# Wide projections of a hybrid GLA/HGRN2 layer: four blocks of 256 columns per job, 512 columns per matmul, in tile pools of their own

## Chip, cores and metric

The kernel runs on one core of one Trainium2 chip. The metric is device time of one execution in microseconds (us), the median of several runs. TensorE is called PE below (its weight loads PEld), VectorE DVE, ScalarE ACT, GpSimd POOL, and SyncE, which issues most of the DMAs, SP.

## What is computed

The reference is one encoder layer on 1024 tokens of width 1024, all in float32. What matters here is its first line: one large projection, whose column blocks are used in different ways.

```
p = jnp.einsum('btd,dp->btp', h, w_in)
(a_q, a_k, a_v, a_gate, a_lr_f, a_lr_b,
 h_q, h_f_f, h_f_b, h_i, h_gate, m_gla, m_hgrn) = _split_columns(p)
...
o_a = head_rmsnorm(o_a, gla_norm_g).reshape(B, T, GLA_V) * jax.nn.silu(a_gate)
y_gla = o_a @ w_branch_gla
...
o_h = head_rmsnorm(o_h, hgrn_norm_g).reshape(B, T, HG_V) * jax.nn.silu(h_gate)
y_hgrn = o_h @ w_branch_hgrn
y = jax.nn.sigmoid(m_gla) * y_gla + jax.nn.sigmoid(m_hgrn) * y_hgrn
return layer_norm(DEEPNORM_ALPHA * h + y @ w_out, ln_g, ln_b)
```

Between the projection and the norms stand two bidirectional chunked recurrences: 4 GLA heads and 8 HGRN2 heads. The four blocks `a_gate`, `h_gate`, `a_v` and `h_i`, 1024 columns each, are the wide projections: their results are wanted with tokens on the partitions.

## The kernel before

**Numbers.** A float32 product is made of three matmuls of the rounded type float32r: each operand is split into a high part (a cast on ACT, line 91) and a low part, what the cast left over (a subtraction on DVE, line 92), and high*high, high*low and low*high are added up in PSUM. So a product over 4 blocks of 128 inner elements takes 12 matmuls for each tile of its output.

**Seven products.** The projection uses Strassen's scheme in Winograd's form. Inputs, tokens and columns are each cut in two, and instead of eight products of quarter size seven are made, P1 to P7, from sums of operand quarters (`sums`) and with sums of results (`seven`, line 1012 for the additions). All seven operands on the side of x are kept in SBUF (`xs`).

**Stage one** is `dense`. It runs 16 narrow jobs and then eight wide ones, and builds the operands of job n+1 (`prepare`) ahead of job n. A narrow job makes two blocks of 128 columns, with weights as the stationary operand and 512 tokens streaming (`narrow_product`, line 975). A wide job makes two blocks of 256 columns, with 128 tokens stationary and 256 columns of weights streaming (`wide_product`, line 988): 7 products of 4 token blocks of 12 matmuls. With the last eight narrow jobs go the GLA decays, one `gla_logs` each: two matmuls (line 1167), then a chain of four ACT passes (lines 1168 to 1171, with two loads of activation tables), three DVE steps (lines 1169, 1172 and the running sum of line 1180) and a store. Halves of the merge gates (`merge_half`, 24 matmuls of 512 columns at line 1315) stand at the start of the stage (0 to 5) and at its end (6 to 8, `STARTED` to `BEGUN`).

**Stage two** is `heads`: 12 heads in the order of `SEQUENCE`, with the rest of the merge gates (`MERGES`, line 1375) and later the GLA branch as work that fills PE in between; a merge gate below `BEGUN` needs one half more, the others both. Stage three is the HGRN branch and the last product (lines 1375 and 1635).

**Order and memory.** The tile framework schedules the instructions of each engine in advance; an engine then runs its queue strictly in that order, and SP its DMAs too. Loads go through SP, in stage one stores go through POOL. Each stage has pools of its own in SBUF, `p0` here: `runs`, `raw` (5 tiles), `s` (3), `w` (8) and `h` (13). When a stage's pools close, the next stage's lie over them, and a new tile waits until the old tiles under it are done with. PSUM has eight banks of 512 columns (`bank`).

Of the kernel before, what the change touches and what calls it, by code (L numbers as in the profile page):

```python
# [9 lines left out]
F32 = mybir.dt.float32  # L10
# [6 lines left out]
P = 128  # L17
# [857 lines left out]
class Fast(Layer):  # L875
# [106 lines left out]
    def wide_product(self, w, x):  # L982
        def product(out, name, more=False):
            a, b = w[name], x[name]
            terms = [(k, i, j) for k in range(4) for i, j in ((0, 0), (1, 0), (0, 1))]
            for c in range(4):
                for n, (k, i, j) in enumerate(terms):
                    self.nc.tensor.matmul(  # L988
                        out[c // 2][:, 256 * (c % 2) : 256 * (c % 2) + 256],
                        b[k][:, j, P * c : P * c + P],  # L990
                        a[i][:, k, :],
                        start=(n == 0 and c % 2 == 0 and not more),
                        stop=(n == len(terms) - 1),
                        skip_group_check=True,
                    )

        return product

# [214 lines left out]
    def wide_job(self, kind, columns, w):  # L1213
        nc = self.nc
        for column in columns:
            self.staged[column] = self.dr.tile([P, NT * 256], F32, name=f"{kind}d")

        def out(i, j, n, c, psum):
            o = 1024 * j + 512 * n
            s = c  # L1220
            if kind == "gate":
                s = self.h()
                nc.scalar.activation(s, c, AF.Sigmoid)
                nc.vector.tensor_tensor(out=s, in0=c, in1=s, op=ALU.mult)
            elif psum:
                s = self.h()
                nc.scalar.copy(s, c)
            self.store(self.staged[columns[i]][:, o : o + 512], s)

        self.seven(self.wide_product(w, self.xs), 2, out)  # L1230

    def dense(self):
# [11 lines left out]
        self.staged = {}  # L1244
# [13 lines left out]
        def block(column):  # L1258
            halves = []
            for n in range(2):  # L1260
                r = self.t("raw", (P, 4, 256))
# [547 lines left out]
```

## Time and profile before

| | us |
|---|---|
| median of three runs | 1408.28 |
| the three runs | 1407.91, 1408.28, 1414.06 |
| the profiled execution | 1407.21 |
| its span | 1405.5 |
| PE busy | 1333.9 |
| DVE busy | 867.5 |
| ACT busy | 670.9 |

The profile is of one execution. A busy PE is not a PE at its peak: matmuls overlap, and what a stream of them costs is read from its length divided by their number, not from the duration of one. The chain of waits is followed back from the last instruction: at each step to what released it. A gap of an engine that the chain doesn't pass costs nothing.

### The profile page before, as it was taken

What the parts mean: (1) busy time and instruction counts of PE and PEld (TensorE: products, weight loads), DVE (VectorE), ACT (ScalarE), POOL (GpSimd) and SP (SyncE); (2) the same over time, 40 slices, a digit from 0 to 9 for tenths busy, and PEclk for the clock granted to TensorE, in tenths of its full rate; (3) what the DMA queues carried; (4) which work ended last, traced back from release to release, by engine and by line L of the source; (5) the groups of instructions that cost most, each with busy time, mean ns of one, the idle gap of its engine ahead of it and who ended that gap; (6) DMA issues with size and microseconds to landing.
All of it is one profiled execution on the core that took longest, in us unless ns stands there. A gap on an engine that the chain in (4) does not pass through costs nothing.

```text
span 1405.5 us, 21115 instructions
## 1 busy us (share of the span) xinstructions
PE 1333.9 (95%) x8009; PEld 1150.1 (82%) x8009; DVE 867.5 (62%) x1434; ACT 670.9 (48%) x1190; POOL 172.6 (12%) x270
## 2 busy tenths in 40 slices
PE   7999989999989999999999999998889999799996
PEld 5888867777889999999987888776677888577885
DVE  8787775797666666444435565567666354675544
ACT  6566565766533333222214565576766455654100
POOL 1134342111111111110010000001000000000011
PEclk9999989999999999999999999999899999899999
DMA  7343433343342333333266353455766241775431
GB/s 277 120 173 137 148 135 119 114 142 120 143 158 97 99 98 121 105 106 111 92 239 221 107 200 112 166 184 191 237 220 211 82 135 53 271 261 172 158 102 52
DMA packets 83153, 210.45 MB, mean 150 GB/s; under 512 B 10656, under 2 KB 10656, under 8 KB 80992
## 3 DMA queue, kind: packets, MB, share of 16 engines
q1 hardware_dynamic: 68368, 160.48, 33.7%
q0 software_dynamic: 14672, 48.51, 9.1%
q8 instruction: 65, 1.06, 0.3%
q14 instruction: 48, 0.39, 0.1%
HBM read 137.65 MB, written 71.30 MB: 149 GB/s over the span
## 4 chain that ended last, share of the span: by engine, by line
PE 74%; DMA 11%; ACT 6%; DVE 5%; issue 3%; POOL 1%; SPq 0%; POOLq 0%; DVEq 0%; ACTq 0%
PE bank L988 22%; PE bank L975 16%; PE proj L1375 13%; PE bank L1635 6%; PE po L566 5%; PE st L566 3%; PE sc L382 2%; DMA raw<-in_dram 2%; PE bank L1315 2%; DMA PF<-logs 2%; DMA hraw<-in_dram 2%; PE bank L1375 2%; DMA g<-ua 1%; DMA g<-sigs 1%; DMA oa<-ot 1%
## 5 line engine op out<-in xcount | busy, mean ns | idle before, releaser
L975 PE MATMUL bank<-xP,w 128*128 128x512 f32 x1344 | 316.9, 396 | 13.5 <-DVE h L1012 8.1
L988 PEld LDWEIGHTS bank<-w,xP 128*128 128x128 f32 x2688 | 323.6, 192 | 0.4
L988 PE MATMUL bank<-w,xP 128*128 128x256 f32 x2688 | 323.5, 283 | 0.0
L975 PEld LDWEIGHTS bank<-xP,w 128*128 128x128 f32 x1344 | 255.3, 191 | 71.5 <-DVE h L1012 9.6
L1375 PE MATMUL proj<-x,hw 128*128 128x512 f32 x576 | 148.5, 402 | 3.0 <-ACT hw L91 1.6
L91 ACT CAST w<-s 128x512 fp32r<-128x512 f32 (+1 forms) x96 | 72.6, 761 | 122.0 <-PE bank L988 71.9
L91 ACT CAST w<-raw 128x512 fp32r<-128x512 f32 (+1 forms) x90 | 65.1, 731 | 131.9 <-PE bank L988 90.7
L1375 PEld LDWEIGHTS proj<-x,hw 128*128 128x128 f32 x576 | 106.1, 190 | 25.1 <-DVE hw L92 1.9
L92 DVE TENSOR_TENSOR w<-s,w 128x512 fp32r<-128x512 f32 (+1 forms) x96 | 83.9, 876 | 56.9 <-ACT w L91 56.7
L1375 PE MATMUL bank<-oh,hw 128*128 128x512 f32 x384 | 91.7, 400 | 9.8 <-ACT hw L91 7.9
L1375 PEld LDWEIGHTS bank<-oh,hw 128*128 128x128 f32 x384 | 73.3, 193 | 28.0 <-ACT hw L91 8.6
L1375 PE MATMUL proj<-xP,hw 128*128 128x512 f32 x360 | 94.3, 402 | 2.0 <-ACT hw L91 1.6
L1012 DVE TENSOR_TENSOR h<-bank,h 128x512 f32<-128x512 f32 x96 | 65.7, 686 | 42.8 <-PE bank L988 35.2
L1528 POOL TENSOR_TENSOR rs<-msall,mhalf 128x4 f32<-128x4 f32 (+1 forms) x32 | 28.4, 887 | 441.2 <-DVE msall L1527 434.8
L92 DVE TENSOR_TENSOR hw<-hraw,hw 128x512 fp32r<-128x512 f32 x64 | 44.0, 688 | 62.2 <-ACT hw L91 62.0
L92 DVE TENSOR_TENSOR w<-raw,w 128x512 fp32r<-128x512 f32 (+1 forms) x90 | 74.7, 837 | 11.9 <-ACT w L91 10.9
L1375 PEld LDWEIGHTS proj<-xP,hw 128*128 128x128 f32 x360 | 65.4, 188 | 17.4 <-ACT hw L91 2.5
L1012 DVE TENSOR_TENSOR h<-h,bank 128x512 f32<-128x512 f32 x65 | 44.5, 685 | 53.7 <-PE bank L988 30.0
L1565 ACT ACTIVATE V<-st,ends 128x128 f32<-128x128 f32 (+1 forms) x168 | 58.4, 421 | 18.9 <-PE st L566 18.7
L566 PE MATMUL st<-v,KT 128*128 128x128 f32 (+1 forms) x336 | 61.0, 324 | 5.5 <-ACT V L1565 5.1
L1315 PE MATMUL bank<-xP,w 128*128 128x512 f32 x216 | 53.8, 412 | 7.9 <-ACT xP L91 6.8
L91 ACT CAST hw<-hraw 128x512 fp32r<-128x512 f32 x64 | 39.8, 623 | 42.9 <-PE proj L1375 25.5
(194 smaller groups left out, 2011.9 us busy)
## 6 DMA issues: line engine op xcount, KB each, us to landing
raw<-in_dram SPq DMA_DIRECT2D x82, 256.0 KB, 3.1
hraw<-in_dram SPq DMA_DIRECT2D x68, 256.0 KB, 3.3
raw<-in_dram SPq DMA_DIRECT2D x33, 512.0 KB, 3.7
ks<-h POOLq DMA_DIRECT2D x40, 256.0 KB, 3.1
K<-ks SPq DMA_DIRECT2D x20, 512.0 KB, 4.8
logs<-h POOLq DMA_DIRECT2D x32, 256.0 KB, 2.7
gated<-h POOLq DMA_DIRECT2D x32, 256.0 KB, 2.7
vd<-h POOLq DMA_DIRECT2D x32, 256.0 KB, 2.7
```

What stands on the lines that cost most here:

```text
L91: nc.scalar.copy(hi, raw)
L92: (lo_engine or nc.gpsimd).tensor_tensor(out=lo, in0=raw, in1=hi.bitcast(F32), op=ALU.subtract)
L382: mm = lambda out, l, r: nc.tensor.matmul(out, l, r, start=True, stop=True)
L566: self.nc.tensor.matmul(out, l, r, start=(i == 0), stop=(i == len(terms) - 1))
L975: self.nc.tensor.matmul(out[0], a[i][:, k, :], b[k][:, j, :], start=(n == 0 and not more), stop=(n == len(terms) - 1), skip_group_check=True,)
L988: self.nc.tensor.matmul(out[c // 2][:, 256 * (c % 2) : 256 * (c % 2) + 256], b[k][:, j, P * c : P * c + P], a[i][:, k, :], start=(n == 0 a ...
L1012: nc.vector.tensor_tensor(out=to[n], in0=one[n], in1=two[n], op=op)
L1315: self.nc.tensor.matmul(ps, w.both[a][:, k, :], xs[k][:, b, :], start=(m == 0), stop=(m == len(terms) - 1))
L1375: nc.tensor.matmul(ps, parts[k][a], self.plain[k, n][:, b, :], start=(m == 0), stop=(m == len(terms) - 1))
L1528: nc.gpsimd.tensor_tensor(out=rs[:, cs], in0=ms, in1=self.mhalf[:, cs], op=ALU.pow)
L1565: nc.scalar.mul(new, u, ends[:, c, near : near + 1])
L1635: nc.tensor.matmul(pss[m], y[:, k, rows], self.wo[k, n][:, j, part], start=(i == 0), stop=(i == len(terms) - 1))
```

## The change

The eight wide jobs become four (`quad_job`), each of four blocks of 256 columns: one quarter of the weights is now 512 columns wide, and a matmul streams 512 columns into a whole bank. The four jobs run in a stage of their own (`wide_stage`, line 1266 for the matmuls), in pools of their own over those of `dense`: `blk` (5 tiles of 4 x 512), `w` (6 tiles, one for each inner block, high and low together), `h` (12) and `g` (2). A product takes its four banks in turn, inner block by inner block; only P3, the last, goes bank by bank. The sums of weights are built in place in `blk` (line 1212). Results are staged with two blocks side by side, so that a store has pieces of 256 elements. The order of the jobs is gate, gate, H_I, A_V instead of gate, gate, A_V, H_I. One more half of a merge gate is made ahead of the heads (four in place of three: 6 in `dense`, 7 to 9 in `wide_stage`), and `MERGES` is shifted by one.

```
-        for start, kind, n in ((A_GATE, "gate", 4), (H_GATE, "gate", 4), (A_V, "v", 4), (H_I, "v", 4)):
-            for b in range(0, n, 2):
-                jobs.append((kind, None, (start + 256 * b, start + 256 * (b + 1))))
...
+    def quad_operands(self, columns):
...
+        def load(i, n):
+            r = block()
+            for m in range(2):
+                src = self.io["ww"][WIDE.index(columns[2 * i + m])]
+                nc.sync.dma_start(out=r[:, :, 256 * m : 256 * m + 256], in_=src[:, 4 * n : 4 * n + 4, :])
+            return r
...
+        def put(raw):
+            tiles = []
+            for k in range(4):
+                u = self.t("w", (P, 2, 512), F32R)
+                self.split(u[:, 0], u[:, 1], raw[:, k])
+                tiles.append(u)
+            return tiles
+
+        a11, a21, a22, a12 = load(0, 0), load(1, 0), load(1, 1), load(0, 1)
+        yield put(a11)
+        s1 = block()
+        sub(s1, a21, a22, ALU.add)
+        sub(a21, a11, a21)
+        sub(a11, s1, a11)
+        yield put(a11)
+        yield put(a12)
+        sub(a12, a12, a11)
+        yield put(a21)
+        yield put(s1)
+        yield put(a22)
+        yield put(a12)
...
+        def out(i, j, n, c, psum):
+            o = 1024 * j + 256 * n
+            s = c
+            if kind == "gate":
+                s = self.t("g", (P, 512))
+                nc.scalar.activation(s, c, AF.Sigmoid)
+                to = s if psum else c
+                nc.vector.tensor_tensor(out=to, in0=c, in1=s, op=ALU.mult)
+                s = to
...
+            self.store(self.pairs[columns[2 * i]][:, :, o : o + 256], s.rearrange("p (m e) -> p m e", e=256))
+
+        def product(banks, name, w, more=False, last=False):
+            terms = [(k, i, j) for k in range(4) for i, j in ((0, 0), (0, 1), (1, 0))]
+            turns = [(c, n) for n in range(len(terms)) for c in range(4)]
+            if last:
+                turns.sort()
+            for c, n in turns:
+                k, i, j = terms[n]
+                nc.tensor.matmul(
+                    banks[c],
+                    self.xs[name][k][:, j, P * c : P * c + P],
+                    w[k][:, i],
...
+    def wide_stage(self):
+        self.counts = {"blk": 5, "w": 6, "h": 12, "g": 2}
+        self.staged, self.pairs = {}, {}
+        for start, kind in ((A_GATE, "gate"), (H_GATE, "gate"), (H_I, "v"), (A_V, "v")):
+            self.quad_job(kind, [start + 256 * b for b in range(4)])
+        for i in range(self.JOINED, self.BEGUN):
+            self.merge_half(i)
...
-        for i in range(self.STARTED, self.BEGUN):
+        for i in range(self.STARTED, self.JOINED):
             self.merge_half(i)
...
-    STARTED, BEGUN = 6, 9
+    STARTED, JOINED, BEGUN = 6, 7, 10
...
-    MERGES = ((9, 10), (11, 0), (12, 1), (13, 2), (14, 3), (15, 4), (5, 6), (7, 8), (), (), (), ())
+    MERGES = ((10, 0), (11, 1), (12, 2), (13, 3), (14, 4), (15, 5), (6, 7), (8, 9), (), (), (), ())
...
-                    self.stage(c, "p0", [["runs"], ["raw"], ["s"], ["w"], ["h"]])
-                    self.dense()
+                    with ExitStack() as n:
+                        self.stage(n, "p0", [["runs"], ["raw"], ["s"], ["w"], ["h"]])
+                        self.dense()
+                    with ExitStack() as n:
+                        self.stage(n, "p0w", [["blk"], ["w"], ["h"], ["g"]])
+                        self.wide_stage()
```

**Place one: PE, from the last narrow job into the wide ones.** The two matmuls of line 1167 are those of the last `gla_logs`; line 975 with xP_160 is the narrow P2, with xP_430 P7, with xP_269 P3; line 988 is a wide matmul. Before:

```order
L1167 MATMUL bank<-w 128x512 x2
L988 MATMUL bank<-w,xP_134 128x256 x2
L975 MATMUL bank<-xP_160,w 128x512 x3
L975 MATMUL bank<-xP_161,w 128x512 x3
L975 MATMUL bank<-xP_162,w 128x512 x3
L975 MATMUL bank<-xP_163,w 128x512 x3
L988 MATMUL bank<-w,xP_134 128x256 x2
L975 MATMUL bank<-xP_430,w 128x512 x3
L975 MATMUL bank<-xP_431,w 128x512 x3
L975 MATMUL bank<-xP_432,w 128x512 x3
L975 MATMUL bank<-xP_433,w 128x512 x3
L988 MATMUL bank<-w,xP_135 128x256 x3
```

In the changed kernel the same two matmuls and the 24 of P2 and P7 follow each other without any wide ones, and then come (line 1393 is a half of a merge gate, line 1266 a wide matmul):

```order
L1393 MATMUL bank<-xP_160,w 128x512 x3
L1393 MATMUL bank<-xP_161,w 128x512 x3
L1393 MATMUL bank<-xP_162,w 128x512 x3
L1393 MATMUL bank<-xP_163,w 128x512 x3
L975 MATMUL bank<-xP_269,w 128x512 x3
L975 MATMUL bank<-xP_270,w 128x512 x3
L975 MATMUL bank<-xP_271,w 128x512 x3
L975 MATMUL bank<-xP_272,w 128x512 x3
L1266 MATMUL bank<-w,xP_134 128x512 x12
L1266 MATMUL bank<-w,xP_135 128x512 x12
L1266 MATMUL bank<-w,xP_136 128x512 x12
```

What fills PE between the last decays and the wide jobs is now 24 matmuls of merge gate 6 and no longer the first wide products, which stand behind all of the narrow stage.

**Place two: SP, the loads of weights at the same point.** The names in brackets are the semaphores that a load waits for: DMASW for a store through POOL, DMAHW for an earlier load. Before, the first wide loads take `raw` tiles in turn:

```order
L1059 DMA raw_2866<-in_2_dram 128x512 [waits DMASW2_49,DVE_49]
L1059 DMA raw_2866<-in_2_dram 128x512
L1262 DMA raw_3023<-in_3_dram 128x1024 [waits DMAHW1_49,DMAHW6_49,DMAHW0_49,DVE_49]
L1262 DMA raw_3025<-in_3_dram 128x1024 [waits DMAHW3_49,DMAHW2_49,DMAHW7_49,DVE_49,Activation_49]
L1262 DMA raw_3027<-in_3_dram 128x1024 [waits DMASW7_49,DVE_49]
L1262 DMA raw_3029<-in_3_dram 128x1024 [waits DMAHW5_49,DMAHW4_49,DVE_49]
```

In the changed kernel (`raw_3144` is merge gate 6, `blk_3222` is a11, `blk_3225` a21, `blk_3228` a22):

```order
L1379 DMA raw_3144<-in_2_dram 128x512 [waits DMAHW6_49,DMASW7_49,DVE_49]
L1379 DMA raw_3144<-in_2_dram 128x512 [waits DMAHW7_49]
L1207 DMA blk_3222<-in_3_dram 128x4x256 [waits DMASW7_49,DMAHW0_49,DMASW2_49,DMAHW1_49,DVE_49,Activation_49]
L1207 DMA blk_3222<-in_3_dram 128x4x256
L1207 DMA blk_3225<-in_3_dram 128x4x256 [waits DMAHW2_49,PE_49]
L1207 DMA blk_3225<-in_3_dram 128x4x256 [waits DMAHW3_49]
L1207 DMA blk_3228<-in_3_dram 128x4x256 [waits DMAHW4_49]
L1207 DMA blk_3228<-in_3_dram 128x4x256 [waits DMAHW5_49]
```

The first wide load now stands for two stores through POOL, the later of which is the store of the last `gla_logs` (its tile lies under `blk_3222`), and all other wide loads are queued behind it.

**Place three: PE at the start of the heads.** Line 1375 (1453 in the changed kernel) is a merge gate, line 382 the first scores of head H0. Before:

```order
L1375 MATMUL proj<-xP_134,hw 128x512 x3
L1375 MATMUL proj<-xP_135,hw 128x512 x3
L1375 MATMUL proj<-xP_136,hw 128x512 x3
L1375 MATMUL proj<-xP_137,hw 128x512 x3
L1375 MATMUL proj<-xP_160,hw 128x512 x2
L1375 MATMUL proj<-x,hw 128x512 x12
L1375 MATMUL proj<-xP_269,hw 128x512 x2
L382 MATMUL sc<-PF,FF 64x128
```

Now:

```order
L1453 MATMUL proj<-xP_269,hw 128x512 x3
L1453 MATMUL proj<-xP_270,hw 128x512 x3
L1453 MATMUL proj<-xP_271,hw 128x512 x3
L1453 MATMUL proj<-xP_272,hw 128x512 x3
L1453 MATMUL proj<-x,hw 128x512 x12
L382 MATMUL sc<-PF,FF 64x128
```

Counted from the first of them, 76 such matmuls stood ahead of the first scores, and now 60 do.

## Rows read from the trace of the kernel before

**Rows 1.** The page: busy time of the engines, and the chain's shares by engine.
```profile
PE 1333.9 (95%) x8009; PEld 1150.1 (82%) x8009; DVE 867.5 (62%) x1434; ACT 670.9 (48%) x1190; POOL 172.6 (12%) x270
...
PE 74%; DMA 11%; ACT 6%; DVE 5%; issue 3%; POOL 1%; SPq 0%; POOLq 0%; DVEq 0%; ACTq 0%
```

**Rows 2.** Stretches: length, PE PEld DVE ACT POOL busy (count), clock, DMA share, GB/s.
```profile
0.00:35.00 35.00, 26.31 (x94) 20.73 (x95) 30.09 (x56) 23.81 (x41) 3.68 (x15) 0.95 0.78 279
...
377.49:397.85 20.36, 16.50 (x93) 14.44 (x93) 16.61 (x17) 11.28 (x13) 2.16 (x4) 0.93 0.37 135
393.53:397.85 4.32, 4.32 (x13) 3.44 (x14) 3.04 (x3) 0.00 (x0) 1.28 (x3) 0.66 0.73 267
397.85:714.00 316.15, 316.15 (x2634) 316.14 (x2633) 174.10 (x199) 89.58 (x114) 34.56 (x64) 1.00 0.33 110
...
760.00:980.00 220.00, 212.63 (x1355) 171.81 (x1354) 131.28 (x289) 136.14 (x296) 15.43 (x19) 0.98 0.44 155
```

**Rows 3.** The chain in order of time: start, length (us), engine, line, count.
```profile
47.00 141.00 PE bank L975 x622
...
397.85 316.10 PE bank L988 x2632
...
1284.23 21.39 PE bank L1375 x92
1305.62 87.68 PE bank L1635 x432
```

**Rows 4.** Timeline of PE at the entry: start, length, idle before and its end.
```profile
376.87 0.62 PE L1167 MATMUL bank<-w 128*128 128x512 f32 x2
...
393.53 4.32 PE L975 MATMUL bank<-xP,w 128*128 128x512 f32 x12 [3.85 <-DVE h L1012]
```

**Rows 5.** Timeline of an earlier `gla_logs`: its second matmul, ACT, DVE, the store.
```profile
334.36 0.39 PE L1167 MATMUL bank<-w 128*128 128x512 f32 x1
...
335.14 0.68 ACT L1168 ACTIVATE raw<-bank,prm 128x512 f32<-128x512 f32 x1
...
340.60 1.23 DVE L1172 TENSOR_TENSOR raw<-raw 128x1024 f32<-128x1024 f32 x1 [2.40 <-ACT raw L1171]
...
344.98 0.54 POOL L921 DMA_DIRECT2D logs<-raw  x1 [2.53 <-DVE raw L1180]
```

**Rows 6.** DMA issues: count, KB each, median us to landing; below them line 1262.
```profile
gated<-h POOLq DMA_DIRECT2D x32, 256.0 KB, 2.7
...
logs<-raw POOLq DMA_DIRECT2D x8, 512.0 KB, 3.0
...
L1262 SPq DMA_DIRECT2D raw<-in_dram x32: 327/328/394, 350.8 to 636.9; - x32
...
DMA to landing us min/median/max: 3.5/3.7/5.7
```

**Rows 7.** Groups by line and form: count, busy us, mean ns, idle before.
```profile
L1012 DVE TENSOR_TENSOR h<-bank,h 128x512 f32<-128x512 f32 x96 | 65.7, 686 | 42.8 <-PE bank L988 35.2 <-PE bank L975 7.3
...
L92 DVE TENSOR_TENSOR w<-raw,w 128x512 fp32r<-128x512 f32 x66 | 45.3, 696 | 6.1 <-ACT w L91 5.1 <-DMA raw<-in_dram 0.9
...
L91 ACT CAST w<-raw 128x512 fp32r<-128x512 f32 x66 | 39.9, 616 | 40.7 <-PE bank L975 20.0 <-PE bank L988 9.2 <-issue 8.4
```

**Rows 8.** Who PE waited for: us in total, times, longest.
```profile
PE bank L975 <- DVE h L1012: 8.1, 3, 3.9
...
PE bank L1315 <- ACT w L91: 1.1, 1, 1.1
```

**Rows 9.** The chain at the start of the heads.
```profile
730.93 8.02 PE proj L1375 x34
...
746.28 3.94 PE proj L1375 x16
750.22 0.36 PE sc L382 x2
...
791.91 4.94 DMA PF<-logs
```

More of the change, by code (lines that the diff above doesn't have):

```diff
@@ L980, in narrow_product @@
         return product
[L982 to L997, printed above, removed]
     def seven(self, product, count, out, early=False):
@@ L1211, in narrow_job, with sub @@
             self.store(self.logs[2 * (GLA_HEADS + at) + i][:, col], s)
-    def wide_job(self, kind, columns, w):
-        nc = self.nc
-        for column in columns:
-            self.staged[column] = self.dr.tile([P, NT * 256], F32, name=f"{kind}d")
+    def quad_operands(self, columns):
+        nc, v = self.nc, self.nc.vector
+        block = lambda: self.t("blk", (P, 4, 512))
+        def load(i, n):
[4 more added lines that the diff above has]
+            return r
+        def sub(to, one, two, op=ALU.subtract):
+            for k in range(4):
+                v.tensor_tensor(out=to[:, k], in0=one[:, k], in1=two[:, k], op=op)
+        def put(raw):
+            tiles = []
+            for k in range(4):
+                u = self.t("w", (P, 2, 512), F32R)
[15 more added lines that the diff above has]
+        yield put(a12)
@@ new lines, in product @@
+        def product(banks, name, w, more=False, last=False):
[9 more added lines that the diff above has]
+                    w[k][:, i],
+                    start=(n == 0 and not more),
+                    stop=(n == len(terms) - 1),
+                    skip_group_check=True,
+                )
@@ new lines, in add @@
+        def add(to, one, two, op=ALU.add):
+            for t, a, b in zip(to, one, two):
+                nc.vector.tensor_tensor(out=t, in0=a, in1=b, op=op)
+        four = range(4)
+        banks = lambda: [self.bank() for _ in four]
+        temps = lambda: [self.h() for _ in four]
+        w = self.quad_operands(columns)
+        x, y = banks(), banks()
+        e, u, v = temps(), temps(), temps()
+        product(x, "P1", next(w))
+        with first():
+            for n in four:
+                nc.scalar.copy(e[n], x[n])
@@ new lines, in quad_job @@
+        product(y, "P6", next(w))
+        with first():
+            add(u, y, e)
+        product(x, "P2", next(w), True)
+        with first():
+            for n in four:
+                out(0, 0, n, x[n], True)
+        product(y, "P7", next(w), True)
+        with first():
+            add(v, y, e)
+        z = banks()
+        product(z, "P5", next(w))
+        with first():
+            add(e, z, v)
+            for n in four:
+                out(1, 1, n, e[n], False)
+        p = banks()
@@ new lines, in quad_job @@
+        product(p, "P4", next(w))
+        with first():
+            add(v, v, p, ALU.subtract)
+            for n in four:
+                out(1, 0, n, v[n], False)
+        product(z, "P3", next(w), True, True)
+        with first():
+            add(u, u, z)
+            for n in four:
+                out(0, 1, n, u[n], False)
+    def wide_stage(self):
[5 more added lines that the diff above has]
+            self.merge_half(i)
@@ L1243, in dense @@
         self.sigs = self.dr.tile([16, P, T], F32, name="sigs")
-        self.staged = {}
         jobs = []
@@ L1253, in dense @@
         narrow = len(jobs)
[L1254 to L1271 removed]
+        def prepare(n):
+            columns = jobs[n][2]
+            return self.pair_sums(self.pair_loads(self.io["wn"], *(NARROW.index(c) for c in columns)))
         nc.sync.dma_start(out=self.prm, in_=self.io["prm"])
```

36 lines of the change are left out of this document (15 added, 21 removed).

## The prediction

> **What bounds the kernel now.** I read the page first, then the chain of waits, then the stretches, and last the timeline where the edit sits. On the page PE is busy 1333.9 of 1405.5 us, and 74% of the chain that ended last is PE [rows 1]. In order of time that chain shows two long unbroken pieces of stage one: 622 narrow matmuls in 141.00 us, and then 2632 of the 2688 wide ones in 316.10 us [rows 3]. In the wide stretch PE is busy for all of its 316.15 us at full granted clock, while DVE works 174 us and ACT 90 us [rows 2]. So there the interval between matmuls alone sets the pace. Ahead of it, at the entry, lie the only long wait (3.85 us) and 12 matmuls that took 4.32 us [rows 4], at a granted clock of 0.66 [rows 2].
>
> **Term 1, the matmuls themselves.** A wide matmul of 256 columns costs 316.10 / 2632 = 120.1 ns; one of 512 columns 141.00 / 622 = 226.7 ns in the narrow jobs [rows 3]. The last product of the kernel is nearest in form (tokens stationary, weights streaming, two banks in turn): 432 matmuls in 87.68 us [rows 3], 96 of them of 256 columns; (87.68 - 96 x 0.1201) / 336 = 226.6 ns. Twice 120.1 is 240.2, so each pair that becomes one instruction saves 13.5 ns. All wide work: 2688 x 120.1 ns = 322.8 us before, 1344 x 226.7 ns = 304.7 us after, **-18.1 us**, all of it on the chain. Four banks in turn occur nowhere in this trace. The slowest long piece of 512 columns is 92 matmuls in 21.39 us, 232.5 ns [rows 3]; with that the term is 7.8 us smaller. I take 226.7, because the row with the nearest form says the same.
>
> **A rule that speaks against it.** These rows show about 13 ns per matmul beyond its columns. The Trainium skill, TensorE: Matmul & The Clock Gate, section Back-to-back issue gap, gives for a full-speed isolated stream columns / 2.4 + 2.5 ns. An estimate from that page is 109.2 and 215.8 ns, which would leave 2.5 ns a pair and 3.4 us in all. By that rule it is the old 120.1 that holds something else, and twice that less 2.5 ns stays: a rival below. The trace disagrees on the fixed part: 13 ns in three different loops.
>
> **Term 2, the moved half of a merge gate.** 24 matmuls of 226.7 ns, 5.4 us, now run ahead of the heads: **+5.4 us** there. Its two loads and four splits sit where SP, ACT and DVE are not late.
>
> **Term 3, the entry.** Count from Z, the end of the two matmuls of the last `gla_logs`, 377.49 in this trace [rows 4]. Before: 20.36 us [rows 2] hold 36 narrow matmuls (8.2 us) and 2688 - 2632 = 56 wide ones (6.7 us), so 5.5 us are lost. Now the first wide load waits for the store of that `gla_logs`, since its tile lies underneath, and every later wide load is behind it in SP's queue. An undisturbed `gla_logs` goes from the end of its second matmul (334.75) to the issue of its store (344.98) in 10.2 us [rows 5]; the store lands after 3.0 us [rows 6]; a11 is two loads of 512 KB, the first 3.7 us [rows 6], the second 1.9 us later at the 279 GB/s of back-to-back loads at the start [rows 2]; its cast 0.7 us [rows 7]. P1 starts at Z + 19.5 us. PE has 60 matmuls until then (24 of P2 and P7, 24 of merge gate 6, 12 of P3), 13.6 us, so it waits 6 us, part of it inside the merge gate, whose casts stand behind the same ACT chain. After such a wait the clock was low: 12 matmuls in 4.32 instead of 2.72 us [rows 4], +1.6. P1 ends at Z + 19.5 + 10.9 + 1.6 = Z + 32.0. P6 needs a21 and a22, the sixth half: 3.7 + 5 x 1.9 = 13.2 us after the store, Z + 26.4, then nine DVE additions of about 0.69 us (6.2) and a cast (0.6): Z + 33.2. P6 starts there; 108 matmuls are done (24.5 us), so 8.7 us are lost, 3.2 more than before: **+3.2 us**. Bounds: loads that land at 3.5 us with all else fully covered give about -2; six halves strictly one after another at the median of 3.7 us put P6 at Z + 42.2, +12; at the longest 5.7 us [rows 6] at Z + 54, +24. I take overlapped loads, since 279 GB/s can't be had one at a time at 512 KB in 3.7 us (142 GB/s).
>
> **Term 4, three seams between jobs.** The next job's P1 takes the banks that P3 has just filled. P3 goes bank by bank, so only its last bank is late: an addition of 0.69 us [rows 7] and the passing of signals, against three matmuls (0.68 us) that P1 can do first. I take 0.4 us a seam, **+1.2 us**. From below 0; from above the longest wait of that kind, 3.9 us [rows 8], three times, 11.7.
>
> **Term 5, the heads.** They lose the 24 matmuls of term 2. Ahead of the first scores stand 60 in place of 76, and between 730.93 and 750.22 the chain is mostly those [rows 9]; from 760 to 980 PE is busy 97% [rows 2]. So most of the 5.4 us comes back, but the chain also passes a load of decays of 4.94 us [rows 9], for which nothing shrinks. Bounds 0 and -5.4; I take **-4.0 us**.
>
> **What costs nothing, and under which cover.** Operands: a gate job has 28 splits, 16 sums, 20 additions and 16 gate products on DVE, 80 x 0.69 = 55 us under 336 x 0.2267 = 76 us of PE; ACT has 48 x 0.62 = 30 us [rows 7]. With six `w` tiles the fourth tile of a product is written once the second block of the product ahead is done, 5.4 us before its end. Gate outputs of P2 have two `g` tiles, so the third bank waits for a store: sigmoid, product, landing of 2.7 us [rows 6], twice over about 8 us, under P7's 10.9. If that cover went, ACT's splits behind the wait would stop PE in each job. Next job's loads wait for tiles freed in P7, P5 and P4, 20 us or more ahead of use. Loads and stores in pieces of 1 KB are shown by no row; their ordinary place is off the chain, at the entry they are in the bounds above. The other order of A_V and H_I only makes H0's values ready sooner.
>
> **The sum.** -18.1 + 5.4 + 3.2 + 1.2 - 4.0 = -12.3 us. The profiled execution took 1407.2 us (span 1405.5 and 1.7 around it), 1.1 us below the median of the runs, less than any bound here. Forecast **1394.9 us**.
>
> **Rivals.**
> (a) The loads at the entry run one after another, or P6 is late for another reason there: +9 us over my entry, 1403.9; with 5.7 us a half 1415. For it: one queue, shorter pieces. Against it: 279 GB/s at the start.
> (b) The heads give nothing back, since they wait for loads: 1398.9.
> (c) The change doesn't do what it says: the saving isn't per instruction, and a 512-column matmul costs 2 x 120.1 - 2.5 = 237.7 ns when its stationary operand is a token block and four banks take turns. 1344 x 11.0 ns = +14.8: 1409.7. Against it 226.7 and 226.6 in two other loops.
> (d) Slower: the operands don't keep up. Half of each product's operand is now written while the product ahead runs, on ACT and DVE queues that also hold evacuations and waits for stores. PE then stops once per product. A wait for a cast was 1.1 us long in the merge halves [rows 8]; 28 x 1.1 = 31 us, 1425.7. It decides from 12.3 / 28 = 0.44 us per product. For it: strict queues, six tiles in place of eight. Against it: the slack of some 4 us per product, and no wait of PE in the old wide stretch.
> (e) Faster: entry covered and the heads return everything, 1386 to 1389.
>
> **How the numbers follow.** Forecast 58% (1389 to 1401), (a) 12%, (b) 10%, (c) 6%, (d) 8%, (e) 6%. The range 1388 to 1406 takes in the forecast, (b), most of (a), some of (e), and leaves out (c), (d) and the tails. Half a per cent, 7 us, is what a measurement of this kernel can tell from no change: below 1401.2 lie the forecast, (b) and (e), 73%; (a) and (c) within it, 19%; (d) beyond, 8%.
>
> **What would show it.** In the changed profile: the matmuls of line 1266 in pieces of the chain at 226.7 ns each (term 1; 237 would be (c)); PE idle ahead of the first of them about 4 us and ahead of the first with xP6 about 1 us, ended by loads of `blk` (term 3); waits at the first P1 of jobs two to four under 1 us, ended by DVE `h` (term 4); waits for `w` elsewhere near none ((d) otherwise); the first scores about 14 us after the last merge half (term 5). Wrong would be, above all, a wait that recurs in every product or every job.

## The result, and the profile after

The changed kernel takes 1387.01 us (median of four runs, 1384.18 to 1390.65), the kernel before in the same comparison 1409.99. The ratio is 0.9851, with a 95% interval of 0.9821 to 0.9882: 21.0 us less (16.6 to 25.2); the two medians differ by 23.0. The forecast was 1394.9 us, 13.4 below the median of before that it was made from, in a range from 1388 to 1406. The direction was right. The gain was about one and a half times as large as forecast, and the median lies 1 us below the low end of the range. The profiled execution took 1384.18 us, with a span of 1382.5.

The page, busy time and the chain by engine (of before: [rows 1]):

```profile
PE 1311.2 (95%) x6665; PEld 1075.8 (78%) x6665; DVE 871.7 (63%) x1524; ACT 680.4 (49%) x1248; POOL 182.9 (13%) x271
...
PE 76%; issue 8%; DMA 8%; ACT 3%; DVE 3%; POOL 1%; SPq 0%; POOLq 0%; DVEq 0%; ACTq 0%
```

There are 1344 matmuls fewer, and PE is 22.7 us less busy, still 95% of the span. The chain in order of time (start, length, engine, line, count; of before: [rows 3]):

```profile
382.56 2.90 DMA logs<-raw
...
386.02 6.17 DMA blk<-in_dram
...
392.94 307.52 PE bank L1266 x1344
```

All 1344 wide matmuls are one unbroken piece. Ahead of it stands the wait that the prediction spoke of: the store of the last `gla_logs`, then the loads of a11. To see where the time went I cut both executions at four points that both programs have. These are the end of the two matmuls of the last `gla_logs` (Z), the first filler of the heads (a filler is a matmul of the merge gates or of the GLA branch that is put between those of the heads), the one matmul of line 848 behind the heads, which belongs to the kernel's own test of the range of the decays, and the first matmul of the last product. Each row gives the stretch, its length, busy time of PE, PEld, DVE, ACT and POOL (count), granted clock, DMA share, GB/s. First before, then the changed kernel:

```profile
7.00:377.49 370.49, 356.69 (x1510) 289.54 (x1511) 280.37 (x396) 226.66 (x330) 90.26 (x138) 0.98 0.42 149
377.49:730.93 353.44, 348.96 (x2796) 343.72 (x2795) 193.90 (x221) 103.74 (x133) 38.34 (x71) 1.00 0.35 118
730.93:1203.80 472.87, 448.35 (x2889) 368.52 (x2889) 272.99 (x616) 278.86 (x625) 28.93 (x33) 0.98 0.47 164
1203.80:1305.46 101.66, 91.88 (x385) 73.61 (x386) 66.70 (x106) 55.52 (x95) 0.00 (x0) 0.93 0.74 251
1305.46:1405.50 100.04, 87.83 (x433) 74.53 (x431) 50.02 (x84) 2.40 (x4) 13.27 (x16) 0.96 0.28 96
```

```profile
7.00:372.33 365.33, 351.64 (x1509) 285.92 (x1510) 280.94 (x396) 226.62 (x331) 90.36 (x138) 0.99 0.41 147
372.33:717.45 345.12, 338.13 (x1477) 278.25 (x1476) 200.34 (x319) 115.20 (x194) 48.31 (x72) 0.99 0.39 129
717.45:1181.70 464.25, 442.95 (x2865) 364.58 (x2865) 270.68 (x606) 277.88 (x622) 29.14 (x33) 0.98 0.48 164
1181.70:1284.50 102.80, 90.67 (x385) 72.54 (x386) 66.44 (x106) 55.37 (x94) 0.00 (x0) 0.95 0.74 248
1284.50:1382.50 98.00, 87.84 (x433) 74.53 (x431) 49.99 (x84) 2.48 (x4) 13.26 (x16) 0.96 0.28 98
```

| stretch | before | after | difference | forecast |
|---|---|---|---|---|
| start to Z | 377.49 | 372.33 | -5.2 | 0 |
| Z to the heads (terms 1 to 4) | 353.44 | 345.12 | -8.3 | -18.1 + 5.4 + 3.2 + 1.2 = -8.3 |
| heads (term 5) | 472.87 | 464.25 | -8.6 | -4.0 |
| between heads and last product | 101.66 | 102.80 | +1.1 | 0 |
| last product to the end | 100.04 | 98.00 | -2.0 | 0 |
| span | 1405.5 | 1382.5 | -23.0 | -12.3 |

The stage that was changed came out as forecast, in this pair of executions to a tenth of a microsecond, with errors in its terms that cancel in part (below). The surplus is in stretches whose work the change hardly touches. The experiments ask which of it is chance and which belongs to the change.

### The profile page after: what moved, and what is told of

Its sections match the earlier page's. It is cut to its first block, busy times and chain, and to the rows that moved or that the text cites. A ratio compares the mean times of both kernels' runs of the same rounds, so it can differ in the third digit from the quotient of the medians.

```text
span 1382.5 us, 18569 instructions
## 1 busy us (share of the span) xinstructions
PE 1311.2 (95%) x6665; PEld 1075.8 (78%) x6665; DVE 871.7 (63%) x1524; ACT 680.4 (49%) x1248; POOL 182.9 (13%) x271
## 4 chain that ended last, share of the span: by engine, by line
PE 76%; issue 8%; DMA 8%; ACT 3%; DVE 3%; POOL 1%; SPq 0%; POOLq 0%; DVEq 0%; ACTq 0%
PE bank L1266 22%; PE proj L1453 14%; PE bank L975 14%; PE bank L1713 6%; PE po L566 5%; PE bank L1393 4%; PE st L566 3%; PE sc L382 2%; PE bank L1453 2%; DMA PF<-logs 2%; DMA hraw<-in_dram 1%; DMA g<-sigs 1%; PE sc L540 1%; DMA g<-ua 1%; PE po L1617 1%
## 5 line engine op out<-in xcount | busy, mean ns | idle before, releaser
L1266 PE MATMUL bank<-w,xP 128*128 128x512 f32 x1344 | 307.5, 391 | 4.8 <-ACT w L91 4.8
L975 PEld LDWEIGHTS bank<-xP,w 128*128 128x128 f32 x1344 | 253.4, 189 | 66.3 <-DVE h L995 5.5
L1266 PEld LDWEIGHTS bank<-w,xP 128*128 128x128 f32 x1344 | 254.0, 189 | 58.2 <-ACT w L91 5.2
L91 ACT CAST w<-blk 128x512 fp32r<-128x512 f32 x118 | 72.5, 623 | 190.4 <-PE bank L1266 165.1
L92 DVE TENSOR_TENSOR w<-blk,w 128x512 fp32r<-128x512 f32 x118 | 80.2, 687 | 99.3 <-ACT w L91 99.2
L1453 PE MATMUL proj<-xP,hw 128*128 128x512 f32 x336 | 91.4, 408 | 1.8 <-ACT hw L91 1.2
L1453 PEld LDWEIGHTS proj<-xP,hw 128*128 128x128 f32 x336 | 61.9, 189 | 15.3 <-ACT hw L91 1.4
L1393 PEld LDWEIGHTS bank<-xP,w 128*128 128x128 f32 x240 | 46.3, 195 | 21.3 <-ACT xP L91 7.7
L91 ACT CAST w<-s 128x512 fp32r<-128x512 f32 x64 | 39.1, 618 | 47.5 <-PE bank L975 37.7
L91 ACT CAST hw<-hraw 128x512 fp32r<-128x512 f32 x64 | 39.5, 619 | 41.6 <-PE proj L1453 23.9
L566 PEld LDWEIGHTS st<-v,KT 128*128 128x128 f32 x336 | 48.7, 196 | 11.9 <-ACT V L1643 6.5
L1713 PE MATMUL bank<-wo,yh 128*128 128x512 f32 (+1 forms) x216 | 53.7, 365 | 0.0
```

Of the source, the lines that this page charges most:

```text
L91: nc.scalar.copy(hi, raw)
L92: (lo_engine or nc.gpsimd).tensor_tensor(out=lo, in0=raw, in1=hi.bitcast(F32), op=ALU.subtract)
L566: self.nc.tensor.matmul(out, l, r, start=(i == 0), stop=(i == len(terms) - 1))
L975: self.nc.tensor.matmul(out[0], a[i][:, k, :], b[k][:, j, :], start=(n == 0 and not more), stop=(n == len(terms) - 1), skip_group_check=True,)
L1266: nc.tensor.matmul(banks[c], self.xs[name][k][:, j, P * c : P * c + P], w[k][:, i], start=(n == 0 and not more), stop=(n == len(terms) - 1 ...
L1393: self.nc.tensor.matmul(ps, w.both[a][:, k, :], xs[k][:, b, :], start=(m == 0), stop=(m == len(terms) - 1))
```

## Experiments

The stretches are timed by the same cuts throughout.

**The two programs again.** Nothing is edited.

> The changed kernel as it is, once more. Its profiled execution was 22.7 us below that of before: 5.2 us of it had gone by before the last gla_logs, where both programs have the same work, 8.3 in the wide stage, 8.6 in the heads, 2.0 behind the last matmul. Theory A (the sum of the prediction holds, the surplus is scatter of single executions: low clock after a stall, landing times at the end): the wide stage, from the last matmul of the last gla_logs to the last matmul of line 1266, again takes 328.1 +- 0.5 us, while the time ahead of it moves between 372 and 378 us and the heads by some us; ratio to before 0.986 to 0.992. Theory B (the surplus belongs to the change, most of it to the heads): the same durations again in every stage, heads from the first merge gate to the last product 567 +- 1 us, ratio 0.983 to 0.986.

> The kernel before, once more, for a second profile of it. Between executions of one program the heads agreed within 1.0 us (567.1 and 568.1 for the changed kernel), between programs with other orders of the heads they lay between 567 and 580. Theory O (the scheduler writes another order of fillers in the heads for each variant, and that order sets the length): heads again 574.5 +- 1 us, and 1.98 us more between the start of the last product and the end of the span than in the changed kernel (99.9 against 98.0). Theory C (chance of the clock): heads anywhere from 567 to 580. The last gla_logs ends somewhere from 372 to 378 us in both.

Heads (and for the first of them the stage from Z) of the changed kernel again and of before again:

```profile
372.93:718.00 345.07, 338.04 (x1477) 278.28 (x1476) 200.44 (x319) 115.17 (x194) 48.22 (x72) 0.99 0.39 129
718.00:1182.50 464.50, 442.97 (x2864) 364.48 (x2864) 270.74 (x606) 276.96 (x622) 29.09 (x33) 0.98 0.48 164
```

```profile
729.30:1203.70 474.40, 448.55 (x2889) 369.67 (x2889) 272.99 (x616) 278.91 (x625) 28.90 (x33) 0.98 0.48 163
```

The ratio of the changed kernel came out at 0.986 (0.9837 to 0.9882), and before again took 1409.63 us. The wide stage repeats to 0.05 us and the heads to 0.3 and 1.5 us, so 8.6 and 9.9 us between the heads of the two programs are no chance of one execution. The 98.0 and 100.0 us at the end repeat too (1384.1 - 1286.1 and 1407.9 - 1307.9). The time up to Z doesn't: 372.9 and 375.4 us here. Over all profiled executions it is 372.3 to 376.7 with the new stage in 512 columns (nine, mean 374.4) and 374.0 to 377.6 in the others (five, mean 376.1), though all run the same work in the same order up to there. Of theory B of these two runs, the part on the heads holds. Ahead of Z, most of the 5.2 us is chance; whether the 1.7 us between the means is more, these few executions don't show. In the expectations the heads were timed to the start of the last product (567.1 and 568.1 us), which takes in the scatter of the stretch behind them.

**One half moved, alone and undone.** Before with `STARTED, BEGUN = 6, 10` and the shifted table; the changed kernel with

```
-    STARTED, JOINED, BEGUN = 6, 7, 10
+    STARTED, JOINED, BEGUN = 6, 7, 9
-    MERGES = ((10, 0), (11, 1), (12, 2), ...
+    MERGES = ((9, 10), (11, 0), (12, 1), ...
```

> The kernel before with one part of the change alone: merge-gate half 9 made ahead of the heads, the table of fillers shifted by one, wide jobs as they were. 24 matmuls (5.4 us) move from the heads to the end of stage one. Theory A (the heads return what they lose and no more): no change, -1.5 to +2 us against before, ratio 0.999 to 1.0015; first scores 5.4 us sooner after the first filler (13.9 in place of 19.3 us). Theory B (the heads gain more than the 24 matmuls, since the fillers fall into other gaps): heads shorter by 7 to 9 us, total -2 to -3.5 us, ratio 0.9975 to 0.9985. Rival (heads wait for loads, nothing comes back): +5 us.

> The changed kernel with that part undone: half 9 and the table of fillers as before, the four wide jobs of 512 columns kept. Theory A: as the changed kernel within 1.5 us, stage one 5.4 us shorter, heads 5.4 us longer. Theory B: 2 to 4 us slower than the changed kernel, all of it in the heads. If the wide jobs are the whole gain, its ratio to before is that of the changed kernel.

Z to the heads and heads, first of before with the half alone, then of the changed kernel with the half back:

```profile
374.04:732.20 358.16, 354.28 (x2822) 348.41 (x2821) 196.68 (x224) 105.72 (x136) 39.02 (x72) 1.00 0.36 120
732.20:1206.30 474.10, 445.08 (x2866) 364.31 (x2864) 272.25 (x614) 279.31 (x623) 29.47 (x33) 0.98 0.47 161
```

```profile
374.92:715.20 340.28, 332.88 (x1453) 273.94 (x1452) 196.37 (x308) 113.15 (x191) 47.96 (x72) 0.99 0.39 126
715.20:1183.40 468.20, 447.46 (x2888) 368.12 (x2888) 273.40 (x616) 277.10 (x624) 28.41 (x33) 0.98 0.48 165
```

Alone, the half gives 1.0019 (0.9998 to 1.0039), 2.7 us that are not clear of no change. In its profiled execution the stage grows by 4.3 to 4.7 us and the heads return nothing (474.1 against 472.9 and 474.4). In the profiles of the changed kernel they return 468.2 - 464.4 = 3.8 us. By the medians they return next to nothing there either: with the half back the kernel takes 1382.54 us, 0.9828 (0.9807 to 0.985), against 1387.11 in the same comparison, 4.6 us less, and the stage is 4.8 us shorter. The profiled execution with the half back was the slowest of its five (1386.17 us), so the 3.8 us may be too high; by these readings what the heads return lies between 0 and 3.8 us. The kernel with the half back has the lowest median of all kernels run. Theory B of these two runs falls: the surplus of the heads doesn't come from the moved half, since with three halves in both kernels they still take 468.2 in place of 472.9 and 474.4.

**256 columns in the new stage.** Pools, jobs, operands and order of products stay.

```
+                for m in range(2):
                     nc.tensor.matmul(
-                        banks[c],
+                        banks[c][:, 256 * m : 256 * m + 256],
...
-                        w[k][:, i],
+                        w[k][:, i, 256 * m : 256 * m + 256],
```

> The changed kernel with each wide matmul made as two of 256 columns into the two halves of its bank: pools, jobs, operands and order of work stay, only the width of the instruction goes back. Theory A (13.5 ns per instruction saved): 2688 x 120.1 = 322.8 us for the wide matmuls, wide stage 346 us in place of 328, total 18 us above the changed kernel, ratio to before 0.997 to 1.001. Rival (c) turned round (the pools and jobs bring the gain, not the width): 113.4 ns per matmul of 256 columns, no difference from the changed kernel. Rule of columns / 2.4 + 2.5 ns: 3.4 us.

The piece of the chain with the wide matmuls, and the two stretches:

```profile
398.45 324.23 PE bank L1267 x2688
```

```profile
377.55:739.70 362.15, 354.87 (x2820) 348.09 (x2819) 201.36 (x319) 114.95 (x194) 48.28 (x72) 1.00 0.37 123
739.70:1210.60 470.90, 441.94 (x2864) 363.78 (x2864) 270.62 (x606) 278.11 (x622) 29.10 (x33) 0.98 0.48 162
```

The ratio is 1.0028 (1.0011 to 1.0045): with narrow instructions nothing of the gain is left, and the new pools and jobs with the moved half cost 1.5 to 6 us. The stage is 17.0 us longer than in the changed kernel, (324.23 - 307.52) / 1344 = 12.4 ns for each pair of instructions that was one, as term 1 had it (13.5). Rival (c) is out. The Trainium skill, TensorE: Matmul & The Clock Gate, section Back-to-back issue gap, leaves 2.5 ns a pair for isolated matmuls, an estimate of 3.4 us in all; these runs disagree. But the medians differ by 1410.97 - 1387.11 = 23.9 us, 7 more than the stage holds, and in the profile the heads are 6.5 us longer than in the changed kernel (470.90 against 464.25 and 464.50). They have the same work, but not the same order: the scheduler wrote the later heads otherwise (below).

**The order of the two value jobs, and of the banks in P3.**

```
-(A_GATE, "gate"), (H_GATE, "gate"), (H_I, "v"), (A_V, "v")
+(A_GATE, "gate"), (H_GATE, "gate"), (A_V, "v"), (H_I, "v")
```

> The changed kernel with the two value jobs in the old order, A_V and then H_I. The orders of all five engines are those of the changed kernel, instruction by instruction; only which columns are made third and which fourth changes. Theory O: every stage as in the changed kernel, heads 567 to 568.5 us, total within 1 us. Rival (H0's values are ready sooner in the changed kernel, and part of the surplus is that): heads 2 to 4 us longer, the wait at their start.

The ratio is 0.9853 (0.9832 to 0.9874), the heads take 1185.0 - 719.8 = 465.2 us: the order of the jobs is worth nothing that can be seen. In the other kernel the two lines `if last: turns.sort()` are taken out.

> The changed kernel with P3 made like the other products, its four banks in turn to the end, not bank by bank; nothing else differs in the order of the engines. At three seams between jobs the next P1 then takes four banks of which none is released before the last four matmuls: it is paced by four additions of 0.69 us, 2.8 us and signals against 0.7 us of matmuls. Term 4 of the prediction (0.4 us a seam bank by bank): three seams at 2.0 to 2.5 us, 5 to 6 us more in all, and twelve waits on DVE h that the changed kernel doesn't have. Rival (the seams are hidden either way): within 1 us.

The stage from Z and the heads, and all that PE waited for at the wide matmuls (line 1264 there):

```profile
374.33:719.40 345.07, 338.18 (x1478) 278.38 (x1476) 200.48 (x319) 116.49 (x194) 48.47 (x72) 0.99 0.39 128
719.40:1180.10 460.70, 439.31 (x2865) 361.65 (x2865) 270.46 (x606) 277.90 (x622) 29.13 (x33) 0.99 0.49 166
```

```profile
PE bank L1264 <- ACT w L91: 4.7, 1, 4.7
```

The ratio is 0.986 (0.9836 to 0.9885), the stage is to 0.05 us the same, and there is no wait at a seam: the rival holds. The prediction had said that the next P1 takes the banks that P3 has just filled. It doesn't. Here are the additions on DVE that read the banks of P4, and then those that read the banks of P3, at the first seam of this kernel:

```profile
464.44 2.48 DVE L1275 TENSOR_TENSOR h<-h,bank 128x512 f32<-128x512 f32 x4
...
474.05 2.48 DVE L1275 TENSOR_TENSOR h<-h,bank 128x512 f32<-128x512 f32 x4
```

The first matmul of the next P1 (the 337th of the stage) starts at 473.76 us, and the next three follow in turn without a wait, while P3's banks are still to be read until 476.53. So P1 takes the other four, those of P4, which had been read by 466.92. The two sets of four alternate in every product, across the seam too, so the banks of a product have the length of a whole one (10.9 us) to come free in. The heads, 460.7 us, show how far one order of instructions scatters: 460.7 to 465.2 over four executions.

**The order of the fillers.** In the orders of PE the later heads exist in two versions. In one, 601 fillers stand ahead of the output of H4; in the other, 30 more have been put into a stretch in which PE otherwise stands idle. All kernels of 256 columns told of above have the first, those of 512 the second. Apart from that the orders differ only in places. Three kernels swap fillers within a head, so that the work of every head stays: all eight pairs of the changed kernel (which gives it the first version too), the fifth pair of before (which gives it the second), and the first pair of the changed kernel (the first).

> The changed kernel with the two fillers of each of the eight heads that have any in the other order, for instance (0, 10) for (10, 0): the same work in every head, stages one and wide untouched. Theory O: the heads come out at another length, by 2 to 10 us away from 567.6, most likely longer, since both other orders that have been seen with four halves ahead took 574 and 580 us. Theory C: 567 to 569 us, and times that differ by under 2 us.

> The kernel before with the two fillers of its fifth head in the other order, (14, 3) to (3, 14): the same work in every head. It makes the scheduler write the second of two orders that have been seen in the heads: in orders of PE, 631 filler matmuls stand ahead of the output of H4 where there were 601 (in all runs of the kernel before, of the half alone and of 256 columns it is the first, in the changed kernel, with half 9 back and in the old order of jobs the second). In the traces the first order leaves PE idle 5.6 to 8.0 us between 300 and 350 us of the heads, the second 2.0 to 3.1. Theory O (that order is what the heads gained beyond the moved half): heads up to the last of them 468 us in place of 472.9 and 474.4, total -4 to -6 us, ratio 0.996 to 0.997. Theory W (the heads gained from the wide stage, through stores and loads): 473 to 474 us, ratio 1.000.

> The changed kernel with the two fillers of its first head in the other order, (10, 0) to (0, 10). It makes the scheduler write the first of the two orders in the later heads, as in the kernel before, with the wide stage of the changed kernel. Theory O: heads 470 to 471 us in place of 464.2 to 465.2, idle 6 to 8 us between 300 and 350 us of the heads, total 5 to 6 us above the changed kernel, ratio to before 0.989 to 0.990. Theory W: 464 to 466 us, ratio 0.985 to 0.986.

The stretch from 300 to 350 us of the heads, where the two versions part: before (first version), before with the second, the changed kernel (second), the changed kernel with the first:

```profile
1030.93:1080.93 50.00, 43.03 (x313) 36.55 (x312) 33.54 (x85) 35.19 (x90) 4.21 (x4) 0.97 0.60 211
```

```profile
1029.90:1079.90 50.00, 46.63 (x321) 39.47 (x320) 30.85 (x70) 36.27 (x93) 2.02 (x2) 0.93 0.63 214
```

```profile
1017.45:1067.45 50.00, 47.93 (x328) 40.63 (x328) 36.43 (x86) 36.99 (x89) 4.03 (x4) 0.97 0.62 217
```

```profile
1020.20:1070.20 50.00, 40.77 (x279) 34.78 (x280) 33.62 (x78) 31.19 (x68) 4.21 (x4) 0.90 0.62 213
```

The idle time there moves as theory O says: PE is idle 7.0 and 9.2 us with the first version, 3.4 and 2.1 with the second. The times don't follow. Before with the second version is 1.0004 (0.9989 to 1.0018), where 0.996 to 0.997 was expected; the changed kernel with the first is 0.9855 (0.9831 to 0.9878), where 0.989 to 0.990 was expected, and all pairs swapped 0.9869 (0.9845 to 0.9893). The heads take 476.3, 468.1 and 464.0 us; the profiled executions of the first two were the slowest of their kernels (1412.34 against a median of 1406.99, 1391.81 against 1388.44), so the ratios weigh more. What one stretch gains is lost in another. Theory O falls as the cause of the surplus: with the first version the heads of 512 columns take 464.0 and 468.1 us, and with the second those of 256 columns 476.3. With it goes the only explanation that I had. Orders other than these two versions were not tried.

**The entry.** Two kernels put more halves of merge gates in front of the waiting P1: `STARTED, JOINED, BEGUN = 6, 10, 10` and `6, 8, 10`.

> The changed kernel with all four halves of merge gates (6 to 9) made at the entry of the wide stage and none at its end: 72 more matmuls (16.3 us) stand between the last gla_logs and the first wide product, which waits 4.8 us there for a load that waits for a store. If that wait and the low clock behind it are all that the entry loses: wide stage with all halves 7 us shorter (Z to the first filler of the heads 338 in place of 345.1). Against it: the four halves need loads through the same queue and tiles of the same pools, so the wait may only move (0), and at its end the heads lose the cover of 16.3 us for their first loads (+3 to +5). Heads in another order of fillers: +-6 us by theory O.

> The changed kernel with two halves of merge gates (6 and 7) at the entry of the wide stage in place of one, and two (8 and 9) in place of three at its end: 24 matmuls (5.4 us) more between the last gla_logs and the first wide product, where PE waited 4.6 to 5.0 us. With none at the end the first scores had waited 18.3 us for loads; two are what the kernel with half 9 back has there, whose wait was 1.2 us. If the wait is covered: from the last gla_logs to the first filler of the heads 340 us in place of 345.1, heads up to 1 us longer, the second order of fillers as in the changed kernel, total -4 us, ratio 0.982 to 0.983. If it only moves (a21 is queued behind the matmuls of half 7, P6 then waits): 345, ratio 0.985 to 0.986.

Timeline of PE (start, length, idle before and its end): with all four halves ahead, the first P1, the last wide matmuls and the first scores; then, with two ahead, P1 and P6:

```profile
411.51 8.68 PE L1266 MATMUL bank<-w,xP 128*128 128x512 f32 x37 [1.19 <-ACT w L91]
...
699.74 16.71 PE L1266 MATMUL bank<-w,xP 128*128 128x512 f32 x73
734.71 0.69 PE L382 MATMUL sc<-PF,FF 128*64 128x128 f32 x2 [18.26 <-DVE PF L1522]
```

```profile
397.80 11.17 PE L1266 MATMUL bank<-w,xP 128*128 128x512 f32 x48 [1.20 <-ACT w L91]
413.80 11.39 PE L1266 MATMUL bank<-w,xP 128*128 128x512 f32 x43 [4.83 <-ACT w L91]
```

Both waits only move. With all four ahead, PE waits 1.2 us for P1. From Z, halves and wide matmuls together take 716.45 - 376.68 = 339.8 us (344.4 in the changed kernel, up to 716.77), and PE then waits 18.3 us for the heads' first loads, which the halves covered before. The ratio is 0.9851 (0.9828 to 0.9873). With two, P1 hardly waits, but a21 is loaded later, and P6 waits 4.8 us: Z to the heads takes 345.9 us, and the ratio is 0.986 (0.9833 to 0.9887). So once the wait for a11 is covered, the loads of a21 and a22 and the sums behind them set the pace at the entry, as the prediction's reckoning of P6 had it.

## Why the prediction was right or wrong, step by step

**Term 1, -18.1 us: right.** Granted clock and count in the first 7 us of the wide matmuls and in the next 70:

```profile
392.94:400.00 7.06, 7.06 (x20) 5.59 (x21) 2.98 (x5) 1.51 (x3) 0.00 (x0) 0.61 1.09 361
400.00:470.00 70.00, 70.00 (x310) 57.95 (x309) 50.17 (x82) 25.48 (x44) 6.88 (x10) 1.00 0.32 102
```

Without the first stretch it is (307.52 - 7.06) / 1324 = 226.9 ns a matmul, where 226.7 was taken from [rows 3]. The row with the nearest form was the right one, and the kernel with 256 columns shows it from the other side. So rival (c), 237.7 ns, didn't come about.

**Term 2, +5.4 us, and term 5, -4.0 us.** The moved half lengthens the stage by 4.8 us (345.1 against 340.3), and the first scores come 731.28 - 716.77 = 14.5 us after the last merge half (about 14 forecast):

```profile
700.29 16.48 PE L1393 MATMUL bank<-xP,w 128*128 128x512 f32 x72
...
731.28 0.43 PE L382 MATMUL sc<-PF,FF 128*64 128x128 f32 x2
```

What the heads return of it is not settled: 3.8 us by the profiles of the changed kernel, next to nothing by its medians, and nothing in the profile of the kernel before with the half alone. The last two speak for rival (b). Since the heads of one order scatter by 4.5 us, 3.8 is no confirmation of the 4.0 that were forecast.

**The step that failed** is the bound of term 5, "0 and -5.4". It took the moved matmuls for all that could change in the heads. They came out 8.6 us shorter, and of that 5 to 6 us (472.9 and 474.4 against 468.2) were there with the half moved back. Nor had the sum a term for the end, where another 2.0 us went.

**What the surplus is.** Ahead of Z, most of the 5.2 us is chance: after the same waits the granted clock fell in one execution and not in the other. Timeline of PE, before and after, and then the stretch of these 12 matmuls in both:

```profile
190.01 4.60 PE L975 MATMUL bank<-xP,w 128*128 128x512 f32 x12 [2.03 <-DVE h L1012]
```

```profile
188.11 3.02 PE L975 MATMUL bank<-xP,w 128*128 128x512 f32 x12 [2.03 <-DVE h L995]
```

```profile
190.01:194.61 4.60, 4.59 (x12) 3.32 (x12) 2.02 (x3) 1.25 (x2) 1.55 (x2) 0.63 0.00 0
```

```profile
188.11:191.13 3.02, 3.02 (x12) 2.17 (x12) 2.02 (x3) 1.24 (x2) 1.55 (x2) 1.00 0.00 0
```

There are four such waits, of 1.9 to 2.2 us, between 188 and 213 us. Behind all four 12 matmuls took 4.3 to 4.6 us in the profile of before, behind two of them in that of after.

The -2.0 us at the end belong to the new stage. The last stretch takes 100.0 us in both executions of before and with the half alone, and 98.0 with the half back and with 256 columns. The difference lies behind the last store, in a drain of POOL, the longest of three. Before and after (count, then shortest, median and longest in ns):

```profile
L1805 POOLq DRAIN  x3: 40/107/5868, 1398.8 to 1405.2; - x3
```

```profile
L1887 POOLq DRAIN  x3: 40/107/1462, 1378.0 to 1382.2; - x3
```

It took 5.87 to 5.95 us in the four profiles without the new stage and 1.38 to 1.46 us in the ten with it, that of 256 columns among them. In the kernel before, the other engines are done 2 us ahead of it; in the changed kernel SP ends after it. Why the drain is shorter, no run shows.

In the heads 3 to 8 us go with the 512 columns: over all profiles they take 470.9 to 476.3 us in the five executions with 256 columns and 460.7 to 468.2 in the eight with 512 that leave halves at the end. Pairs with the same work and the same version of the order are 470.9 against 468.1 and 464.0 (first version), and 476.3 against 468.2 (second, with the half back). Most of it is time in which PE is idle (length less busy time): 24.5 to 29.0 us in the five executions, 20.7 to 24.8 in the eight. Not its cause are the moved half, the order of the value jobs and the seams; which of the two versions of the fillers' order is run moves that idle time but not the total. Each kernel of 512 columns also differs from each of 256 in some places of the order in the heads, and that alone was not tried. **What is its cause stays open.**

**Term 3, the entry, +3.2 us: right in mechanism, a little small.** Timeline of PE, and below it SP and ACT:

```profile
371.72 0.61 PE L1150 MATMUL bank<-w 128*128 128x512 f32 x2
372.17 5.60 PE L975 MATMUL bank<-xP,w 128*128 128x512 f32 x24
378.72 0.74 PE L1393 MATMUL bank<-xP,w 128*128 128x512 f32 x2 [0.94 <-ACT w L91]
380.07 5.39 PE L1393 MATMUL bank<-xP,w 128*128 128x512 f32 x22 [0.62 <-DVE w L92]
385.30 2.88 PE L975 MATMUL bank<-xP,w 128*128 128x512 f32 x12
392.94 7.40 PE L1266 MATMUL bank<-w,xP 128*128 128x512 f32 x20 [4.76 <-ACT w L91]
```

```profile
385.59 9.28 SPq L1207 DMA_DIRECT2D blk<-in_dram  x8
```

```profile
392.27 2.18 ACT L91 CAST w<-blk 128x512 fp32r<-128x512 f32 x4 [6.18 <-DMA blk<-in_dram]
```

The store of `gla_logs` was to be issued at Z + 10.2 and set out at Z + 10.2 (382.56). P1 was to start at Z + 19.5 and started at Z + 20.6, because a11's two halves took 6.6 us from issue to landing and not 5.6. Lost are 20.6 - 13.6 = 7.0 us ahead of P1 and 7.06 - 20 x 0.2267 = 2.5 behind it at a clock of 0.61: 9.5 in place of 8.7, and 4.0 more than before. Rival (a) didn't come about: the six halves overlapped (361 GB/s in the row above), and P6 didn't wait. It started at Z + 34.2, right behind P1; the prediction had it wait 1.2 us, until Z + 33.2.

**Term 4, the seams, +1.2 us: wrong premise.** They cost nothing, since P1 of the next job takes the banks of P4. The two errors of terms 3 and 4 are 0.8 and 1.2 us and cancel almost. With term 1 at 226.9 ns a matmul and term 2 at 4.8, the terms as measured are -17.8 + 4.8 + 4.0 + 0 = -9.0 us, against -8.3 between the first two profiles and -8.8 between the second two. So that -8.3 came out to a tenth is luck, and that it came out within a microsecond is not.

**What was to cost nothing, and rival (d).** PE waited once in 1344 matmuls, at the entry:

```profile
PE bank L1266 <- ACT w L91: 4.8, 1, 4.8
```

So rival (d), a wait in every product, didn't come about: six `w` tiles are enough, and the covers that were named held. The wait for the two `g` tiles is there, on ACT, and short (group by line and form: count, busy, mean ns, idle before):

```profile
L1250 ACT ACTIVATE g<-bank 128x512 f32<-128x512 f32 x8 | 4.6, 599 | 5.2 <-DMA gated<-g 3.7 <-PE bank L1266 1.4
```

**The sum.** In the changed stage -8.3 us were measured for -8.3 forecast. In the heads -8.6 were measured for -4.0, of which about 5 is a part that no term had; at the end -2.0, for which there was no term either. The rest of the difference between the two profiled executions is, for the most part, chance ahead of Z. The range had been drawn around the terms, with nothing for stretches in which the change had no term. The measured 1387.01 us lies where rival (e) stood (1386 to 1389), but not by its mechanism: the entry wasn't covered, it cost 4.0 us more than before, and nothing shows that the heads returned all of the moved half. The prediction's shares also have a small slip: the forecast, (b) and (e) add up to 74% and not 73, (a) and (c) to 18% and not 19.

## What to carry to other kernels

In this kernel, where PE sets the pace and every matmul loads its weights, the price per instruction was read from two loops of different width in the same trace, and it carried over to a third: 13.5 ns forecast and 12.4 measured for each instruction that is saved. A stage downstream whose order is written by a scheduler can change in length with a change upstream (here by 3 to 8 us, for a reason that stays open), so its scatter between programs, not only between executions, belongs in the range. Moving work ahead of a stage is worth only what that stage returns: here 0 to 3.8 us of the 4.8 that it cost, and the kernel without that part of the change has the lower median (1382.54 against 1387.11 us). And a single profile can be the slowest execution of its kernel: compare stretches with the medians at hand.

## What the runs showed of the hardware that was not expected

After one and the same wait of 2.03 us the granted clock fell in some executions and not in others (0.63 and 1.00 over the next 12 matmuls), so that these took 4.60 or 3.02 us; with four such places, the time up to Z varied between 372.3 and 377.6 us in one program order. After the wait of 4.76 us at the entry the granted clock was 0.61 over 7.06 us, so mostly the lower of its two levels (1.2 and 2.4 GHz), and 1.00 after that. The longest drain of POOL took 5.87 us without the new wide stage and 1.46 with it, and in the kernel before this drain alone set the end of the kernel. And the idle time of PE in the heads, behind the wide stage, was 24.5 to 29.0 us with 256 columns there and 20.7 to 24.8 with 512; no run here says why.
